# Expert weights of a one-core decoder trunk stored in pairs of blocks and loaded 2 MB at a time

## The chip, the cores and the metric

The kernel runs on one core of one Trainium2 chip. The time is the device time of an execution in microseconds (us): from the first to the last instruction, and the little that lies around that. TensorE (PE in the profile, PEld its weight loads), VectorE (DVE), ScalarE (ACT), GpSimd (POOL) and SyncE (SP) run their own streams of instructions and wait for each other by semaphores. SP issues almost all DMAs, and 16 DMA engines move their data.

## The reference

A decoder trunk of two layers on 256 tokens with a width of 1024, in float32. Layer 0 is latent attention and a dense SwiGLU, layer 1 a diagonal state-space mixer (S5) and a mixture of 8 experts, of which each token takes two:

```python
def moe_swiglu(h, w_router, w_gate, w_up, w_down):
    t = h.reshape(B * S, D)
    logits = (t @ w_router).astype(jnp.float32)
    top_vals, top_idx = lax.top_k(logits, TOP_K)
    gates = jax.nn.softmax(top_vals, axis=-1)
    combine = jnp.sum(jax.nn.one_hot(top_idx, N_EXPERTS) * gates[..., None], axis=1)
    for e in range(N_EXPERTS):
        out = out + combine[:, e:e + 1] * swiglu(t, w_gate[e], w_up[e], w_down[e])
```

Each expert has three matrices of 1024 x 3584, 42 MB in float32 (MB stands for 1,048,576 bytes), and all eight are read: 336 MB.

## The kernel before

**Blocks and places.** `pack` (L1575) stores an expert as 42 blocks of 128 partitions x 2048 values, 1 MB each, in rows of 8 KB. Blocks lie in the order of use: a chunk of 512 hidden columns takes four blocks for gate and up (`up`, L1248) and two for down (`down`, L1339). Expert 0 is split otherwise: its first and last chunks have 256 columns, two blocks up and one down. `seq` (L1431) runs up of a chunk, then down of the chunk before it. `fetch` (L190) loads each block into the next place of a list, `self.rings`, and SP issues that load when the place's last reader is done. In the expert stage the list has 18 places of 1 MB (L1496, L1438): six tiles that the S5 mixer used before (`KEEP`: M0 to M3, E and F), two of pool `ring2`, four of `ring`, the two halves of the router's transposed input (`gh`, `gl`), and the four pairs of split tiles (`whi`, `wlo`, 512 KB each), which take a block as two DMAs with rows of 4 KB (L202; the others are issued at L205). The list is rotated and the last six places join it after `dense` (L1288), the first chunk's up. Before that there are twelve.

**Early loads.** During S5 three blocks are loaded into M0, M1 and M2 as soon as steps S1, S3 and S5 have read these tables (`PF`, L50; `early`, L183, issued at L187). SP's stream there also holds the last weights of S5 (`in_s_glu`, L205) and small copies (`tt<-kk`, L902).

**Token slices.** An expert's tokens, at most 96 or 64 (`CAPS`, L83), stand in slices of 32 (three or two). Every block takes 48 matmul records of 32 x 256 with three slices, 32 with two. The experts come as 96, 64, 96, 96, 64, 96, 96, 64. Between experts stand `scatter` and, for each second one, `gather`.

**Split places.** Up to the first chunk of the experts, weights are split into a rounded part `whi` (ACT, L227) and the rest `wlo` (DVE, L229), and `mm3` (L251) takes three matmuls (L253 to L255). `split` (L216) works two to three parts ahead of the matmuls.

The order of instructions on each engine follows the program, with shifts that the tile framework's scheduler makes.

Of the kernel before, what the change touches and what calls it, by code (L numbers as in the profile page):

```python
# [19 lines left out]
P = 128  # L20
# [28 lines left out]
KEEP = ("M0", "M1", "M2", "M3", "E", "F")  # L49
PF = "S1:M0 S3:M1 S5:M2"  # L50
# [26 lines left out]
RING, RING2, LOOK = 4, 2, 2  # L77
# [25 lines left out]
class Trunk:  # L103
    def __init__(self, ctx, tc, a, out):
# [4 lines left out]
        self.rings = [(pool("ring", bufs=RING), "w")] * RING  # L109
# [55 lines left out]
    def plan_moe(self):  # L165
        a = self.a
        self.expert = {}
        u = 100000 * (1 + len(self.parts))
        ups, downs = [], []
        for e in range(NE):  # L170
            n = 0
            for w in CHUNKS[e]:
                ups.append([(e, n + i) for i in range(w // 128)])
                n += w // 128
                downs.append([(e, n + i) for i in range(w // 256)])
                n += w // 256
        for x, y in zip(ups + [[]], [[]] + downs):
            for e, n in x + y:
                u += 1
                src = a["moe_w"][0, n] if e == 0 else (e, n)  # L180
                self.parts += [(u, src, 0, 1024), (u, src, 1024, 2048)]

    def early(self, tag):  # L183
        u, src, _, _ = self.parts[self.marks["moe"] + 2 * self.nearly]
        self.nearly += 1
        t = self.keep.tile([P, UNIT], F32, tag=tag, name="w")
        self.nc.sync.dma_start(t, src)  # L187
        self.units[u] = t

    def fetch(self):  # L190
        while self.seen < min(self.cap, self.ahead + self.reach):
            u, src, c0, c1 = self.parts[self.seen]
            if u not in self.units:
                k = max(p[3] for p in self.parts[self.seen:self.seen + 8] if p[0] == u)
                if isinstance(src, tuple):
                    src = self.chosen(*src)
                q, tag = self.rings[self.nunit % len(self.rings)]
                self.nunit += 1
                if isinstance(tag, tuple):
                    t = [q.tile([P, UNIT // 2], F32, tag=z, name="w") for z in tag]  # L200
                    for i in range(2):
                        self.nc.sync.dma_start(t[i], src[:, i * UNIT // 2:(i + 1) * UNIT // 2])  # L202
                else:
                    t = q.tile([P, UNIT], F32, tag=tag, name="w")
                    self.nc.sync.dma_start(t[:, :k], src)  # L205
                self.units[u] = t
            self.seen += 1

    def chosen(self, e, n):

        if e not in self.expert:
# [4 lines left out]
    def split(self):  # L216
        nc = self.nc
        while self.ahead < min(len(self.parts), self.stop) and self.ahead <= self.pos + self.look:
# [5 lines left out]
            hi = sp.tile([P, 1024], F32R, tag="whi", name="whi")  # L224
            lo = sp.tile([P, 1024], F32R, tag="wlo", name="wlo")
# [17 lines left out]
    def raw(self):  # L243
# [4 lines left out]
        w = self.units[u]  # L248
        return w[c0 // 1024] if isinstance(w, list) else w[:, c0:c1]
# [491 lines left out]
    def s5_tables(self, m, t):  # L741
# [63 lines left out]
        E = self.keep.tile([P, G, NCK], F32, tag="E", name="E")  # L805
        F = self.keep.tile([P, G, NCK], F32, tag="F", name="F")
# [22 lines left out]
        self.M = [self.keep.tile([P, 16, P], F32, tag=f"M{i}", name=f"M{i}") for i in range(4)]  # L829
# [233 lines left out]
    def route(self, h, m, rest):  # L1063
# [15 lines left out]
        self.gbuf = [m.tile([P, KB, 2, P], F32R, tag=n, name=n) for n in ("gh", "gl")]  # L1079
# [109 lines left out]
    def experts(self, h, m, half):  # L1189
# [204 lines left out]
        def spare(name):  # L1394
            while isinstance(self.rings[self.nunit % len(self.rings)][1], tuple):
                self.nunit += 1
            q, tag = self.rings[self.nunit % len(self.rings)]
            self.nunit += 1
            return q.tile([P, UNIT], F32, tag=tag, name=name)
# [33 lines left out]
        if half == 0:  # L1433
# [4 lines left out]
            self.rings = self.rings[i:] + self.rings[:i] + [(m, "gh"), (m, "gl")] + [(q, ("whi", "wlo")) for q in self.sps]  # L1438
# [30 lines left out]
def trunk_kernel(ctx: ExitStack, tc: tile.TileContext, a, out, stage=9):  # L1469
# [20 lines left out]
    with tc.tile_pool(name="moe", bufs=1, reuse_waits="tile") as m, \  # L1490
# [5 lines left out]
        t.rings = [(t.keep, k) for k in KEEP] + [(r2, "w")] * RING2 + t.rings  # L1496
# [6 lines left out]
        t.moe(h, m, rest)  # L1503


def pack(inputs):
# [68 lines left out]
    o["moe_w"] = w  # L1575
# [18 lines left out]
```

## Time and profile before

| what | value |
|---|---|
| median of 3 runs | 1346.38 us (1344.81 to 1353.78) |
| the profiled execution | 1347.12 us, its span 1345.3 us |
| granted TensorE clock, mean | 0.970 |
| PE busy | 1270.8 us (94%) |
| DVE, ACT, POOL busy | 499.1, 314.6, 48.5 us |
| moved by DMA | 424.26 MB (of 1,000,000 bytes), mean 315 GB/s |
| expert weights | 264 DMAs of 1 MB and 144 of 512 KB |

The expert stage is the stretch from about 450 us to the end. The profile gives, for any stretch, each engine's busy time, the mean busy share of the 16 DMA engines and what they moved (GB/s of 10^9 bytes). The share is a sum of packet times, and neighbours overlap a little, so 1.01 or 1.02 is an engine that never rests. PE's busy time counts modelled ends of pipelined matmuls: a busy PE is not a PE at its peak, and its pace is read from the start times of its records.

### The profile page before, as it was taken

Reading aid. Unit: us, or ns where it says so; the run is one execution under the profiler, and the core shown is the slowest. Engines: PE = TensorE matmul, PEld = TensorE weight load, DVE = VectorE, ACT = ScalarE, POOL = GpSimd, SP = SyncE. Lnnn points to the kernel's source line nnn. Section 1 sums busy time; section 2 is a strip of 40 time slices with the busy share of each in tenths; the row PEclk is TensorE's granted clock in tenths of the full one; section 3 lists DMA queues with packets and bytes.
Section 4 is the critical chain, followed back from the end, with each engine's and each line's share of the span. In section 5 each row is a group of like instructions: output and inputs, shape, how many; then the busy total and the mean of one; then the engine's idle time right before and its main releaser. Section 6 shows DMA issues by size and latency. Waiting matters only on the chain. (4 is left out here: it accounts for less than half of the span.)

```text
span 1345.3 us, 39012 instructions
## 1 busy us (share of the span) xinstructions
PE 1270.8 (94%) x17355; PEld 883.4 (66%) x17355; DVE 499.1 (37%) x1088; ACT 314.6 (23%) x628; POOL 48.5 (4%) x89
## 2 busy tenths in 40 slices
PE   6998999999789899999999999999999999999984
PEld 6777999998677676666555665555655555666542
DVE  5875989987878760102011002002102002000202
ACT  5664544455433450100010000001000001000001
POOL 3000000001033100000000000000000000000000
PEclk9989999999976899999999999999999999999998
DMA  7302455554445779999999999999999999999994
GB/s 277 135 33 105 157 188 189 196 177 169 154 112 151 252 278 407 415 414 415 416 416 416 419 412 403 418 410 399 415 419 408 407 411 407 415 407 418 409 398 169
DMA packets 80448, 424.26 MB, mean 315 GB/s; under 512 B 14608, under 2 KB 18448, under 8 KB 39824
## 3 DMA queue, kind: packets, MB, share of 16 engines
q1 hardware_dynamic: 76016, 418.79, 78.5%
q0 software_dynamic: 1024, 1.31, 0.7%
q8 instruction: 138, 2.26, 0.7%
q10 hardware_dynamic: 3232, 1.58, 0.5%
q14 instruction: 38, 0.31, 0.1%
HBM read 417.19 MB, written 1.05 MB: 311 GB/s over the span
## 5 line engine op out<-in xcount | busy, mean ns | idle before, releaser
L1246 PE MATMUL pg<-w,xg 128*32 128x256 f32 (+1 forms) x7168 | 494.1, 378 | 4.9 <-DMA w<-in_moe_w 4.9
L1246 PEld LDWEIGHTS pg<-w,xg 128*32 128x32 f32 x7168 | 264.4, 110 | 159.2 <-issue 11.8
L1336 PE MATMUL py<-w,th 128*32 128x256 f32 x4704 | 281.4, 379 | 5.9 <-DMA w<-in_moe_w 5.7
L1282 DVE TENSOR_TENSOR sl<-pg,sl 128x256 f32<-128x256 f32 (+1 forms) x56 | 23.7, 423 | 671.9 <-ACT sl L1281 671.9
L1246 PE MATMUL pu<-w,xg 128*32 128x256 f32 (+1 forms) x2240 | 230.1, 376 | 1.6 <-issue 1.6
L1336 PEld LDWEIGHTS py<-w,th 128*32 128x32 f32 x4704 | 160.6, 110 | 106.9 <-DMA w<-in_moe_w 6.7
L1281 ACT ACTIVATE sl<-pg 128x256 f32<-128x256 f32 (+1 forms) x56 | 21.4, 383 | 651.9 <-PE pg L1246 651.9
L229 DVE TENSOR_TENSOR wlo<-w,whi 128x1024 fp32r<-128x1024 f32 (+1 forms) x120 | 141.3, 1181 | 45.4 <-ACT whi L227 45.0
L227 ACT CAST whi<-w 128x1024 fp32r<-128x1024 f32 (+1 forms) x120 | 121.6, 1019 | 126.2 <-PE pg L254 52.1
L1246 PEld LDWEIGHTS pu<-w,xg 128*32 128x32 f32 x2240 | 102.1, 110 | 48.8 <-issue 3.0
L254 PE MATMUL pg<-n1l,whi 128*128 128x256 f32 x352 | 101.6, 289 | 0.0
L255 PE MATMUL pg<-n1h,wlo 128*128 128x256 f32 x352 | 101.4, 288 | 0.0
L253 PE MATMUL pg<-n1h,whi 128*128 128x256 f32 x352 | 101.3, 288 | 0.1
L253 PEld LDWEIGHTS pg<-n1h,whi 128*128 128x128 f32 x352 | 67.4, 192 | 1.2 <-ACT whi L227 0.3
L254 PEld LDWEIGHTS pg<-n1l,whi 128*128 128x128 f32 x352 | 67.5, 192 | 0.7
L255 PEld LDWEIGHTS pg<-n1h,wlo 128*128 128x128 f32 x352 | 67.4, 192 | 0.0
L253 PE MATMUL fo<-whi,th 128*128 128x512 f32 x88 | 34.6, 393 | 0.3 <-ACT th L700 0.3
L254 PE MATMUL fo<-wlo,th 128*128 128x512 f32 x88 | 34.5, 392 | 0.0
L255 PE MATMUL fo<-whi,tl 128*128 128x512 f32 x88 | 34.3, 389 | 0.0
L1423 POOL TENSOR_TENSOR fx<-h,gF 128x512 f32<-128x512 f32 x1 | 1.3, 1266 | 881.1 <-DVE h L1421 881.1
L1284 DVE STREAM_TRANSPOSE th<-sl 128x384 f32<-128x384 f32 (+2 forms) x56 | 29.4, 525 | 2.0
L1223 ACT ACTIVATE xg<-pgt,prm 128x192 f32<-128x192 f32 x32 | 11.7, 418 | 62.6 <-PE pgt L1218 62.6
(478 smaller groups left out, 1396.1 us busy)
## 6 DMA issues: line engine op xcount, KB each, us to landing
w<-in_moe_w SPq DMA_DIRECT2D x264, 1024.0 KB, 17.1
w<-in_moe_w SPq DMA_DIRECT2D x144, 512.0 KB, 13.6
w<-in_ffn_gu SPq DMA_DIRECT2D x22, 1024.0 KB, 4.8
w<-in_ffn_dn SPq DMA_DIRECT2D x11, 1024.0 KB, 4.8
w<-in_s_glu SPq DMA_DIRECT2D x8, 1024.0 KB, 5.8
w<-in_mla_o SPq DMA_DIRECT2D x4, 1024.0 KB, 4.8
w<-in_s_in SPq DMA_DIRECT2D x4, 1024.0 KB, 4.7
w<-in_mla_in SPq DMA_DIRECT2D x4, 672.0 KB, 8.9
```

The source lines that it names most:

```text
L227: nc.scalar.copy(hi[:, :k], w[:, c0:c1])
L229: self.lo_dve = nc.vector.tensor_sub(lo[:, :k], w[:, c0:c1], hi[:, :k].bitcast(F32))
L253: mm(out, lhsT=lh, rhs=rh, start=first, stop=False)
L254: mm(out, lhsT=lh, rhs=rl, start=False, stop=False)
L255: mm(out, lhsT=ll, rhs=rh, start=False, stop=last)
L1223: self.g_act = nc.scalar.activation(x[:, q + i], src, AF.Copy, scale=gc)
L1246: mm(ps[t // 2][32 * q:32 * q + 32, t % 2, 0:w], lhsT=lhsT, rhs=rhs[:, q], start=first and t % 2 == 0, stop=last and (t % 2 == 1 or t == n ...
L1281: self.silu = nc.scalar.activation(sl[:, ts], src[:, :, 0:k], AF.Silu)
L1282: v.tensor_tensor(sl[:, ts], src[:, :, k:2 * k], sl[:, ts], op=ALU.mult)
L1284: v.transpose(th.rearrange("p t b x -> p (t b x)"), sl.rearrange("p t k -> p (t k)"))
L1336: mm(y[e][b][32 * q:32 * q + 32, i, :], lhsT=th[:, t, fb], rhs=w[:, c * 256:(c + 1) * 256], start=first and i == 0, stop=last and (nt == 2 ...
L1423: (nc.gpsimd, v)[n if XM else 1].tensor_mul(x[:, 1, s], h[:, 1, s], gF[:, s])
```

## The change

- `pack` stores two consecutive blocks side by side, in rows of 16 KB. In expert 0 the two single down blocks are moved behind the others, so that the rest pairs up (`stored`).
- The places become five double ones of 2 MB (M0 with M1: `MA`; M2 with M3: `MB`; E with F: `EF`; one of `ring2`; `gh` with `gl`: `gg`) and eight single ones: four of `ring`, and the four split places, in each of which `whi` and `wlo` are now the halves of one tile `ws`.
- A double place takes a pair in one DMA. A single place, or a double one that meets the second block of a pair or a block of no pair, takes half a pair: rows of 8 KB out of 16.
- Two pairs are loaded early, after S3 and S7, in place of three blocks after S1, S3 and S5.

```diff
-KEEP = ("M0", "M1", "M2", "M3", "E", "F")
-PF = "S1:M0 S3:M1 S5:M2"
+KEEP = ("MA", "MB", "EF")
+PF = "S3:MA S7:MB"
-RING, RING2, LOOK = 4, 2, 2
+RING, RING2, LOOK = 4, 1, 2
...
+    def place(self, name="w"):
+        q, tag, n = self.rings[self.nunit % len(self.rings)]
+        self.nunit += 1
+        return q.tile([P, n * UNIT], F32, tag=tag, name=name), n
...
     def early(self, tag):
-        t = self.keep.tile([P, UNIT], F32, tag=tag, name="w")
-        self.nc.sync.dma_start(t, src)
-        self.units[u] = t
+        t = self.keep.tile([P, 2 * UNIT], F32, tag=tag, name="w")
+        self.nc.sync.dma_start(t, self.chosen(e, k))
+        self.units[u], self.units[u + 1] = t[:, 0:UNIT], t[:, UNIT:2 * UNIT]
...
+                    e, p, i, pair = src
+                    src = self.chosen(e, p)
+                    if pair and n == 2:
+                        self.nc.sync.dma_start(t, src)
+                        self.units[u], self.units[u + 1] = t[:, 0:UNIT], t[:, UNIT:2 * UNIT]
+                    else:
+                        self.units[u] = t[:, 0:UNIT]
+                        self.nc.sync.dma_start(t[:, 0:UNIT], src[:, i * UNIT:(i + 1) * UNIT])
...
-            hi = sp.tile([P, 1024], F32R, tag="whi", name="whi")
-            lo = sp.tile([P, 1024], F32R, tag="wlo", name="wlo")
+            ws = sp.tile([P, UNIT], F32R, tag="ws", name="ws")
+            hi, lo = ws[:, 0:1024], ws[:, 1024:UNIT]
...
-            self.rings = self.rings[i:] + self.rings[:i] + [(m, "gh"), (m, "gl")] + [(q, ("whi", "wlo")) for q in self.sps]
+            self.rings = self.rings[i:] + self.rings[:i] + [(m, "gg", 2)] + [(q, "ws", 1) for q in self.sps]
...
-        t.rings = [(t.keep, k) for k in KEEP] + [(r2, "w")] * RING2 + t.rings
+        t.rings = [(t.keep, k, 2) for k in KEEP] + [(r2, "w", 2)] * RING2 + t.rings
...
+def stored(e):
+
+    return [n for n in range(NUNIT) if e or n not in (2, NUNIT - 1)] + ([] if e else [2, NUNIT - 1])
...
-    o["moe_w"] = w
+    o["moe_w"] = c(np.stack([w[e][stored(e)].reshape(NUNIT // 2, 2, P, UNIT).transpose(0, 2, 1, 3).reshape(NUNIT // 2, P, 2 * UNIT) for e in range(NE)]))
```

## Rows read from the trace of the kernel before

**Rows 1.** Busy time by stretch: the expert stage
```profile
core 0: us, PE busy (x) PEld busy (x) DVE busy (x) ACT busy (x) POOL busy (x), PEclk, DMA share, GB/s
505.00:1320.00 815.00, 801.76 (x14114) 476.94 (x14106) 97.46 (x216) 58.56 (x153) 0.00 (x0) 1.00 1.01 411
```
**Rows 2.** Matmuls of the last blocks, in order of time
```profile
start us, us, engine line op out<-in xcount [idle before <-releaser]
...
1323.02 1.93 PE L1336 MATMUL py<-w,th 128*32 128x256 f32 x32 [0.59 <-DMA w<-in_moe_w]
1325.39 1.93 PE L1336 MATMUL py<-w,th 128*32 128x256 f32 x32 [0.43 <-DMA w<-in_moe_w]
```
**Rows 3.** Busy time of L1246 (PE, PEld) by expert: 1, 2, 4 and 7
```profile
608.00:689.70 81.70, 54.76 (x915) 31.59 (x910) 1.00 1.01 417
689.90:802.70 112.80, 79.41 (x1379) 45.85 (x1374) 1.00 1.02 415
...
923.30:1002.60 79.30, 51.69 (x870) 29.63 (x864) 1.00 1.01 412
...
1238.10:1326.90 88.80, 48.57 (x806) 26.31 (x798) 1.00 0.96 386
```
**Rows 4.** Matmuls of expert 1 (two slices): two downs, one chunk apart
```profile
625.78 3.61 PE L1336 MATMUL py<-w,th 128*32 128x256 f32 x60
...
636.14 3.61 PE L1336 MATMUL py<-w,th 128*32 128x256 f32 x60
```
**Rows 5.** SP's waits, 510 to 600 us
```profile
engine line waited for: us in total, times, longest us
SPq L205 <- PE pu L1246: 43.1, 20, 2.9
SPq L205 <- PE py L1336: 14.0, 7, 2.2
```
**Rows 6.** DMA issues (KB each, median us to landing); a DMA queue (packets, MB, share)
```profile
w<-in_moe_w SPq DMA_DIRECT2D x264, 1024.0 KB, 17.1
w<-in_moe_w SPq DMA_DIRECT2D x144, 512.0 KB, 13.6
...
q8 instruction: 138, 2.26, 0.7%
```
**Rows 7.** Busy time by stretch: rows of 8 KB, then of 4 KB
```profile
516.00:548.00 32.00, 32.00 (x600) 19.30 (x596) 3.44 (x13) 4.09 (x7) 0.00 (x0) 1.00 1.01 421
549.00:561.00 12.00, 12.00 (x228) 7.27 (x224) 1.20 (x3) 0.66 (x2) 0.00 (x0) 1.00 1.02 407
```
**Rows 8.** Busy time by stretch: a slow piece of the stream
```profile
828.00:836.00 8.00, 8.00 (x156) 4.82 (x152) 0.95 (x3) 0.05 (x1) 0.00 (x0) 1.00 0.96 355
```
**Rows 9.** Busy time by stretch: before the first expert chunk
```profile
480.00:504.00 24.00, 23.51 (x179) 17.17 (x182) 15.21 (x61) 13.91 (x32) 0.00 (x0) 1.00 0.64 221
```
**Rows 10.** SP's issues around the end of S5, in order of time
```profile
398.53 0.33 SPq L187 DMA_DIRECT2D w<-in_moe_w  x1
...
438.83 10.84 SPq L902 DMA_DIRECT2D tt<-kk  x8
449.72 2.54 SPq L205 DMA_DIRECT2D w<-in_s_glu  x2
...
453.26 31.87 SPq L205 DMA_DIRECT2D w<-in_moe_w  x10
489.85 3.81 SPq L202 DMA_DIRECT2D w<-in_moe_w  x4
```
**Rows 11.** The weight split: groups of the page (busy, mean ns, idle before)
```profile
L227 ACT CAST whi<-w 128x1024 fp32r<-128x1024 f32 (+1 forms) x120 | 121.6, 1019 | 126.2 <-PE pg L254 52.1
...
L255 PE MATMUL pg<-n1h,wlo 128*128 128x256 f32 x352 | 101.4, 288 | 0.0
...
L253 PEld LDWEIGHTS pg<-n1h,whi 128*128 128x128 f32 x352 | 67.4, 192 | 1.2 <-ACT whi L227 0.3
```

More of the change, by code (lines that the diff above doesn't have):

```diff
@@ L108, in __init__ @@
         self.small = pool("small", bufs=2)
-        self.rings = [(pool("ring", bufs=RING), "w")] * RING
+        self.rings = [(pool("ring", bufs=RING), "w", 1)] * RING
         self.nunit, self.lo_gate = 0, None
@@ L165, in plan_moe @@
     def plan_moe(self):
-        a = self.a
         self.expert = {}
@@ L194, in fetch @@
                 k = max(p[3] for p in self.parts[self.seen:self.seen + 8] if p[0] == u)
[L195 to L202, printed above, removed]
-                else:
-                    t = q.tile([P, UNIT], F32, tag=tag, name="w")
-                    self.nc.sync.dma_start(t[:, :k], src)
-                self.units[u] = t
+                t, n = self.place()
+                if not isinstance(src, tuple):
+                    self.units[u] = t
+                    self.nc.sync.dma_start(t[:, :k], src)
+                else:
+                    e, p, i, pair = src
[6 more added lines that the diff above has]
+                        self.nc.sync.dma_start(t[:, 0:UNIT], src[:, i * UNIT:(i + 1) * UNIT])
             self.seen += 1
     def chosen(self, e, n):
+        if e == 0:
+            return self.a["moe_w"][0, n]
         if e not in self.expert:
@@ L247, in raw @@
         self.pos += 1
-        w = self.units[u]
-        return w[c0 // 1024] if isinstance(w, list) else w[:, c0:c1]
+        return self.units[u][:, c0:c1]
     def mm3(self, out, lh, ll, rh, rl, first, last):
@@ L804, in s5_tables @@
         yield
-        E = self.keep.tile([P, G, NCK], F32, tag="E", name="E")
-        F = self.keep.tile([P, G, NCK], F32, tag="F", name="F")
+        EF = self.keep.tile([P, 2, G, NCK], F32, tag=KEEP[2], name="EF")
+        E, F = EF[:, 0], EF[:, 1]
         self.E, self.F = E, F
@@ L828, in s5_tables @@
                             yield
-        self.M = [self.keep.tile([P, 16, P], F32, tag=f"M{i}", name=f"M{i}") for i in range(4)]
+        M = [self.keep.tile([P, 2, 16, P], F32, tag=z, name=z) for z in KEEP[0:2]]
+        self.M = [M[i // 2][:, i % 2] for i in range(4)]
         for b in range(8):
@@ L1078, in route @@
         nc.gpsimd.tensor_copy(tri, self.cst[:, C_TRI:C_TRI + P])
-        self.gbuf = [m.tile([P, KB, 2, P], F32R, tag=n, name=n) for n in ("gh", "gl")]
+        gg = m.tile([P, 2, KB, 2, P], F32R, tag="gg", name="gg")
+        self.gbuf = [gg[:, 0], gg[:, 1]]
         xh, xl = self.x3 = [z.rearrange("p k a t -> p k (a t)") for z in self.gbuf]
@@ L1394, in spare @@
         def spare(name):
[L1395 to L1399, printed above, removed]
+            return self.place(name)[0][:, 0:UNIT]
         def final_start():
```

13 lines of the change are left out of this document (6 added, 7 removed).

## The prediction, made before the change was run

> **What bounds the kernel now.** I read the strip of 40 slices first: from about 500 us on the DMA row stands at 9 to the last slice. So the busy time by stretch comes next: from 505 to 1320 us the DMA engines' share is 1.01, at 411 GB/s, and the clock is 1.00 [rows 1]. 411 GB/s are 2.551 us per MB, and the stream never rests. PE is busy all the time as well, so the third view has to be its pace. Per expert [rows 3], one of three slices takes 112.8 us (expert 2), 2.69 us per MB, slower than the stream. One of two slices can go faster: from one down to the next, which is one chunk or 6 MB, expert 1 takes 636.14 - 625.78 = 10.36 us, 1.73 us per MB [rows 4]. So the blocks in SBUF pile up in three-slice experts and are eaten in two-slice ones. Where the pile is gone PE goes at the stream's pace: each group of matmuls for the last blocks has 0.4 to 0.6 us of idle before it, released by a weight DMA [rows 2]. Expert 7 takes 88.8 us, where 42 MB at 1.73 us and some 3.5 us for the scatter (an estimate: what expert 2's 112.8 us leave over 42 MB at 1.5 x 1.73, three slices for two) make 76. Expert 4 takes 79.3. PE thus waits for data some 13 + 3 = 16 us, and the execution ends when the stream does. That is the limit for any gain from the stream: 1347.1 - 16 = 1331 us.
>
> SP's waits show the other end of the pile: in expert 0 SP waits 57 of 90 us for PE to give places back [rows 5], while the stream, with its issued loads, still runs.
>
> **The loads themselves.** In a stretch that moves rows of 8 KB alone the stream makes 421 GB/s, in one of 4 KB rows (the split places) 407 [rows 7]. Per row on one of 16 engines that is 8192 x 16 / 421 = 311.3 ns and 4096 x 16 / 407 = 161.0 ns: 150.3 ns for 4 KB more, and 10.7 ns for each row whatever its size. A row of 16 KB on the same line is 611.9 ns, so 2 MB (eight rows per engine) take 4.895 us, 2.448 us per MB; 1 MB in 8 KB rows takes 2.491, in 4 KB rows 2.576.
>
> Before: 264 x 2.491 + 72 x 2.576 = 843.1 us [rows 6]. After: a lap of 13 places holds 18 blocks, five pairs and eight single; 336 blocks are 18.7 laps, so 93 pairs and 150 single: 93 x 4.895 + 150 x 2.491 = 828.9 us. The difference is 14.2 us. 16 of the 336 MB lie before 505 us, where the stream is not the limit, which leaves 13.5. 72 x 0.085 = 6.1 us of the 14.2 come from the 4 KB rows that go, 186 x 0.043 = 8.0 from the 16 KB rows.
>
> No row shows a weight load of 16 KB rows, so its price has two ends. Below: no cost per row, 601 ns, 8 us more gained. Above: the only queue with packets of that size, the instruction queue (2.26 MB in 138), has 0.007 x 16 x 1345 / 138 = 1.09 us per packet [rows 6], which would add 93 x 3.8 = 355 us. Its packets share the engines with weight packets, which would be in their time too; I take the line through the two sizes of the same queue. Between the ends stands a row cut into two packets of 8 KB, 2.491 us per MB.
>
> The stream's slow pieces stay as they are: 355 GB/s over 8 us [rows 8], and the 13 us between 815 us and the 802 that 320 MB would take at the rates of [rows 7]. Nothing in the change touches them.
>
> What the Trainium skill says of a load's fixed cost ("DMA: Bandwidth & Descriptors", the anatomy of one DMA on the SWDGE path) is about 2.0 us for each, whatever its size. The change issues 165 DMAs less, so by that sentence alone it would save up to 330 us. The trace disagrees for this queue: loads take 13.6 and 17.1 us to land while the share stays at 1.01 [rows 1, 6], so what is fixed lies under other loads. If the 0.085 us per MB between the two rates of [rows 7] belonged to the additional DMA and not to the shorter rows, 165 fewer would save 14.0 us, the same sum.
>
> **The start.** From 480 to 504 us the share is 0.64 [rows 9]: 8.6 us of rest, because places are full. The change takes one place from this stretch: block 6, expert 0's single down, sits alone in the double `ring2` place, so 11 blocks fit where 12 did. And `MA` comes free only when both its blocks are split, which is when the last of the ten issues of [rows 10] went out (453.26 + 31.87 = 485.1), and not one block earlier as M0 did. Against it stands one more MB loaded early. About 4.5 us more rest, 2.5 less to load: 2 us lost. Bounds: 2.5 gained (the places give the same rest as now) to 5 lost (`MB`, which needs two blocks of the first chunk consumed, holds SP's queue up).
>
> **The end.** The last two blocks are one pair now. After its landing 64 records remain where 32 do now: 1.9 us [rows 2] minus the wait saved, 1.7 us lost. Below zero it cannot go; the bound above is one load, 2.5.
>
> **Early loads in S5.** Two loads of 4.9 us at S3 and S7 replace three of 2.5 at S1, S3 and S5. The one at S7 lands on SP's queue beside the last copies (438.83 to 449.67) and before two S5 weights at 449.72 [rows 10], which wait behind it for up to 4.9 us. Their split begins later than that, and PE works on earlier parts meanwhile. I take 0; bounds 2.5 gained (a load less beside the small copies) and 4.9 lost if that cover is gone.
>
> **Joined split places.** ACT waits for the place 52.1 us in all, released by L254, the last reader of `whi` [rows 11]. With one tile it is released by L255, at most 288 ns later, in 44 parts of the dense layer: 12.7 us if nothing covered it. PE's weight load of `whi` shows 1.2 us of idle in all 352, so two parts in advance cover it: 0. Fewer issues on SP: 0, it waits anyway.
>
> **Sum.** -13.5 + 2 + 1.7 = -9.8 us on the profiled execution's 1347.1: 1337.3. That execution is 0.7 us above the median, so I say 1337. PE has 16 us to give, and 9.8 are taken: the end stays with the stream.
>
> **Rivals.**
> A, the forecast, 1337 (its own range 1331 to 1343): chance 0.52.
> B, 16 KB rows move as two packets: 336 x 2.491 = 837.0, 5.8 us saved after 505 us, less 3.7 lost: 1345. For it: no 16 KB row of this queue is seen. Against: the instruction queue has packets of that size. 0.13.
> C, the long rows cost nothing per row, or the start loses nothing: the stream runs away and PE's own pace ends it, 1331. Against: [rows 7] show a cost per row. 0.13.
> D, slower: depth. A double place comes back only when both blocks are used, and a pair can be used only when 2 MB have landed. That is about 0.5 MB held, 1 MB later, 1 MB in the half-empty place: 2.5 to 3 MB less of a pile of 18, 7.5 us at 2.5 us per MB in each of the two eating stages (experts 4 and 7), 15 us: 1337 + 15 = 1352. For it: SP waits for places in expert 0 already [rows 5]. Against: the stream's share stays at 1.0 there. It decides once the pile at the start of expert 4 is under some 12 MB. 0.15.
> E, slower: longer rows meet in memory. Neighbouring partitions lie 16 KB apart, so the engines' streams are 64 KB apart where they were 32. If pairs went at the 355 GB/s of [rows 8], each would take 5.91 us in place of 4.90: 93 x 1.01 = 94 us, 1431; it costs more than it gives from 5.05 us a pair on. Against: half blocks of 4 KB at a pitch of 8 KB go at 407, on the line. 0.07.
> The skill's same page, under latency and other measured facts, has such a loss for row pitches from 512 KiB up (207 GB/s there, 103 at 4 MiB), far above 16 KB; no run here shows it.
>
> **Chances and range.** A measurement tells about 1% from no change here: 1333 and 1360 are the marks. Faster by more: C mostly (0.10) and A's lower end (0.08), 0.18. Slower by more: E and a bad D, 0.09. Within: 0.73. The range 1329 to 1353 holds A, B, C and most of D.
>
> **What would show it.** Right: DMA share 1.0 from 505 us on; 428 GB/s where pairs alone move and 421 in single places, none at 407; 93 issues of 2 MB and 150 of 1 MB; expert 4 at 76 to 77 us, expert 7 near 80; PE's waits for weights halved. Rest in 480 to 504 of about 13 us. Wrong: a rate of 421 throughout with twice the packets (B); shares under 0.95 in expert 0 or more than 16 us of PE waits (D); under 415 GB/s in stretches of pairs (E); first expert matmul later than 501 us (the S5 loads).

## The result, and the profile after

The changed kernel takes 1357.49 us (median of 15 runs, 1353.05 to 1360.94), the kernel before 1348.36 us beside it (15 runs, 1344.81 to 1354.08). The ratio is 1.0065, with a 95% interval of 1.0052 to 1.0079: slower by some 9 us, where 10 us less was forecast. The profiled execution after takes 1353.05 us, the lowest of its 15, with a span of 1351.3 us; the span before is 1345.3, so the two profiles differ by 6.0 us where the medians differ by 9.1.

The stream of weights did nearly what the change wanted. Busy time by stretch, for the stretches of [rows 9], [rows 1] and [rows 7], and the first 80 us after these:

```profile
480.00:504.00 24.00, 24.00 (x127) 17.69 (x126) 17.89 (x63) 11.61 (x24) 0.00 (x0) 1.00 0.57 201
505.00:1320.00 815.00, 808.49 (x14188) 485.23 (x14191) 100.86 (x222) 65.44 (x168) 0.00 (x0) 1.00 1.00 416
516.00:548.00 32.00, 32.00 (x580) 19.24 (x571) 3.03 (x8) 2.29 (x7) 0.00 (x0) 1.00 1.00 411
...
520.00:600.00 80.00, 80.00 (x1481) 48.00 (x1473) 8.49 (x27) 7.33 (x16) 0.00 (x0) 1.00 0.99 404
```

The whole stage goes from 411 to 416 GB/s, though its beginning is slower (404 GB/s from 520 to 600 us; this is the line before):

```profile
520.00:600.00 80.00, 78.38 (x1547) 49.03 (x1539) 7.04 (x22) 6.08 (x13) 0.00 (x0) 1.00 1.01 417
```

The DMA issues of the page, to be held against [rows 6], and the packets between 505 and 1320 us (56011 before):

```profile
w<-in_moe_w SPq DMA_DIRECT2D x93, 2048.0 KB, 23.0
w<-in_moe_w SPq DMA_DIRECT2D x150, 1024.0 KB, 22.8
```

```profile
DMA packets 33672, 338.70 MB, mean 416 GB/s; under 512 B 3735, under 2 KB 3735, under 8 KB 3799
```

93 pairs and 150 single blocks, as counted. In this stretch 89 pairs and 142 singles are issued, at 128 rows each 29568 packets; with the 3.8 thousand small ones that makes 33.4 of the view's 33.7 thousand. A row of 16 KB is one packet. The experts, busy time of L1253 by stretch, for experts 1, 2, 4 and 7 as in [rows 3]:

```profile
618.70:700.70 82.00, 54.15 (x915) 31.74 (x911) 1.00 1.00 421
700.90:813.70 112.80, 79.41 (x1380) 45.86 (x1374) 1.00 1.01 422
933.50:1014.30 80.80, 53.10 (x868) 30.27 (x864) 0.98 1.01 421
1248.40:1332.30 83.90, 48.34 (x806) 25.48 (x798) 0.96 0.89 370
```

The stream makes 421 to 422 GB/s where it made 412 to 417. Expert 7 falls from 88.8 to 83.9 us, expert 4 does not fall (79.3 to 80.8). PE's waits for weights, 4.9 + 5.7 us on the page before, are halved, as the page's groups show (after the bar busy time, mean ns, idle before):

```profile
L1253 PE MATMUL pg<-w,xg 128*32 128x256 f32 (+1 forms) x7168 | 494.3, 379 | 2.5 <-DMA w<-in_moe_w 2.5
...
L1343 PE MATMUL py<-w,th 128*32 128x256 f32 x4704 | 280.6, 381 | 2.7 <-DMA w<-in_moe_w 2.7
...
L233 ACT CAST ws<-w 128x1024 fp32r<-128x1024 f32 (+1 forms) x120 | 121.5, 1019 | 123.6 <-PE pg L260 31.2
...
L258 PEld LDWEIGHTS pg<-n1h,ws 128*128 128x128 f32 x352 | 67.3, 191 | 1.4 <-ACT ws L233 0.5
```

The last two lines answer to [rows 11]: the joined split tile is released by L260, the last reader of `lo`, and nothing waits noticeably longer for it.

So the loss lies ahead of the stage. The first expert matmul starts at 500.4 us before and at 511.5 after; the last ends at 1327.3 and 1332.6. The stage is thus 5.8 us shorter (826.9 to 821.1), and all else is lost earlier. In S5, counted from block 0's output (its first `py<-tt` matmul, 377.4 and 374.4 us; other profiled executions here have it between 374 and 380) to the first expert matmul, 123.0 us became 137.1. SP's issues in that stretch, to be held against [rows 10]:

```profile
start us, us, engine line op out<-in xcount [idle before <-releaser]
394.55 0.33 SPq L190 DMA_DIRECT2D w<-in_moe_w  x1
404.06 4.91 SPq L908 DMA_DIRECT2D tt<-kk  x4
413.44 0.33 SPq L874 DMA_DIRECT2D bc<-in_s5bc  x1
416.48 0.33 SPq L876 DMA_DIRECT2D dd<-in_s_dd  x1
416.86 0.67 SPq L874 DMA_DIRECT2D bc<-in_s5bc  x1
...
431.81 2.52 SPq L908 DMA_DIRECT2D tt<-kk  x4
...
445.84 0.33 SPq L190 DMA_DIRECT2D w<-in_moe_w  x1
446.41 10.34 SPq L908 DMA_DIRECT2D tt<-kk  x8
457.21 0.34 SPq L201 DMA_DIRECT2D w<-in_s_glu  x1
```

Two things are to be seen. Each early load of 2 MB stands directly ahead of small copies (`tt<-kk`, the local operators of the S5 blocks). And the loads of table rows (`bc`, L874), one of which SP issued at 402.26 us before, ahead of block 3's copies, now stand behind them at 413.44 us. SP's issues before, behind the early load of 398.53 us [rows 10]:

```profile
402.26 0.33 SPq L868 DMA_DIRECT2D bc<-in_s5bc  x1
402.64 0.42 SPq L205 DMA_DIRECT2D w<-in_s_glu  x1
405.90 4.94 SPq L902 DMA_DIRECT2D tt<-kk  x4
```

Two of SP's longest waits in the changed kernel, from 374 to 470 us:

```profile
engine line waited for: us in total, times, longest us
...
SPq L908 <- DMA X<-ut: 12.2, 4, 9.0
...
SPq L190 <- PE pS L937: 9.6, 1, 9.6
```

The early load at S7 is at the head of SP's queue for 9.6 us until PE has read `MB`, with the last eight copies behind it. And the copies of block 3 wait 9.0 us at the head for small copies of ScalarE's queue (`X<-ut`), which were issued beside the first load. How long DMAs took from issue to landing, 394 to 404 us in the changed kernel:

```profile
w<-in_moe_w SPq DMA_DIRECT2D x1, 2048.0 KB, 8.3
X<-ut ACTq DMA_DIRECT2D x8, 16.0 KB, 6.8
tt<-kk POOLq DMA_DIRECT2D x1, 64.0 KB, 4.2
```

PE stands still for them, in order of time:

```profile
402.08 1.06 PE L928 MATMUL pU<-cst,X 32*128 32x32 f32 x8 [5.66 <-DMA w<-in_moe_w]
```

The matmul belongs to block 4 and reads `X`. The last of the eight copies that fill this `X` was issued at 394.62 us, 0.07 us behind the load, and took 7.1 us, to 401.7. (The profile names the load as what ended the wait, but that landed only at 402.9.) Before, the same matmul waited for the same copy for 1.04 us:

```profile
399.24 1.04 PE L922 MATMUL pU<-cst,X 32*128 32x32 f32 x8 [1.04 <-DMA X<-ut]
```

### The profile page after: what moved, and what is told of

Its sections match the earlier page's. It is cut to its first block, busy times and chain, and to the rows that moved or that the text cites. A ratio compares the mean times of both kernels' runs of the same rounds, so it can differ in the third digit from the quotient of the medians.

```text
span 1351.3 us, 38357 instructions
## 1 busy us (share of the span) xinstructions
PE 1270.0 (94%) x17355; PEld 885.0 (65%) x17355; DVE 499.9 (37%) x1088; ACT 314.1 (23%) x628; POOL 47.9 (4%) x89
## 3 DMA queue, kind: packets, MB, share of 16 engines
q0 software_dynamic: 1024, 1.31, 0.6%
## 5 line engine op out<-in xcount | busy, mean ns | idle before, releaser
L1253 PE MATMUL pg<-w,xg 128*32 128x256 f32 (+1 forms) x7168 | 494.3, 379 | 2.5 <-DMA w<-in_moe_w 2.5
L1253 PEld LDWEIGHTS pg<-w,xg 128*32 128x32 f32 x7168 | 264.9, 110 | 157.6 <-issue 12.5
L1253 PE MATMUL pu<-w,xg 128*32 128x256 f32 (+1 forms) x2240 | 230.9, 377 | 1.4 <-issue 1.4
L1343 PEld LDWEIGHTS py<-w,th 128*32 128x32 f32 x4704 | 163.5, 110 | 100.9 <-issue 4.4
L235 DVE TENSOR_TENSOR ws<-w,ws 128x1024 fp32r<-128x1024 f32 (+1 forms) x120 | 141.4, 1184 | 42.4 <-ACT ws L233 41.7
L233 ACT CAST ws<-w 128x1024 fp32r<-128x1024 f32 (+1 forms) x120 | 121.5, 1019 | 123.6 <-PE pg L260 31.2
L1253 PEld LDWEIGHTS pu<-w,xg 128*32 128x32 f32 x2240 | 102.4, 110 | 49.1 <-issue 3.4
L259 PE MATMUL pg<-n1l,ws 128*128 128x256 f32 x352 | 101.5, 288 | 0.0
L260 PE MATMUL pg<-n1h,ws 128*128 128x256 f32 x352 | 101.4, 288 | 0.0
L258 PE MATMUL pg<-n1h,ws 128*128 128x256 f32 x352 | 101.1, 287 | 0.3 <-ACT ws L233 0.3
L258 PEld LDWEIGHTS pg<-n1h,ws 128*128 128x128 f32 x352 | 67.3, 191 | 1.4 <-ACT ws L233 0.5
L259 PEld LDWEIGHTS pg<-n1l,ws 128*128 128x128 f32 x352 | 67.3, 191 | 0.7
L260 PEld LDWEIGHTS pg<-n1h,ws 128*128 128x128 f32 x352 | 67.3, 191 | 0.0
L258 PE MATMUL fo<-ws,th 128*128 128x512 f32 x88 | 34.5, 392 | 0.0
L259 PE MATMUL fo<-ws,th 128*128 128x512 f32 x88 | 34.5, 392 | 0.0
L260 PE MATMUL fo<-ws,tl 128*128 128x512 f32 x88 | 34.3, 390 | 0.0
```

The source lines that it names most:

```text
L233: nc.scalar.copy(hi[:, :k], w[:, c0:c1])
L235: self.lo_dve = nc.vector.tensor_sub(lo[:, :k], w[:, c0:c1], hi[:, :k].bitcast(F32))
L258: mm(out, lhsT=lh, rhs=rh, start=first, stop=False)
L259: mm(out, lhsT=lh, rhs=rl, start=False, stop=False)
L260: mm(out, lhsT=ll, rhs=rh, start=False, stop=last)
L1253: mm(ps[t // 2][32 * q:32 * q + 32, t % 2, 0:w], lhsT=lhsT, rhs=rhs[:, q], start=first and t % 2 == 0, stop=last and (t % 2 == 1 or t == n ...
```

## The experiments

Theory T1: the two early loads lengthen S5. Rival T2: the joined tiles and the order of instructions that came with them do, whatever is loaded. T3: S5 aside, the half-empty and late places at the start of the stage eat the gain. T4 and T5 came when T1 had to be split: by order (table loads behind copies) or by bytes (small copies landing behind 2 MB). All lengths below are from the profiled execution of each kernel, read from its timeline in the same way; times are medians, ratios are against the kernel before run beside it.

| kernel | time, us | ratio, 95% interval | S5, us | stage, us |
|---|---|---|---|---|
| before | 1348.4 | 1 | 123.0 | 826.9 |
| changed | 1357.5 | 1.0065 (1.0052 to 1.0079) | 137.1 | 821.1 |
| changed, no early loads | 1339.4 | 0.9938 (0.9914 to 0.9962) | 120.0 | 822.6 |
| before, four early loads of 1 MB | 1356.3 | 1.0072 (1.0047 to 1.0096) | 130.5 | 825.7 |
| changed, first four places single | 1346.0 | 0.9985 (0.9970 to 1.0000) | 124.2 | 822.0 |
| before, no early loads | 1352.9 | 1.0033 (1.0016 to 1.0051) | 124.0 | 830.1 |
| changed, S3 load only | 1355.7 | 1.0048 (1.0028 to 1.0068) | 137.4 | 820.9 |
| changed, early loads in halves | 1355.5 | 1.0041 (1.0015 to 1.0067) | 142.3 | 818.7 |
| no early loads, pairs in halves | 1345.1 | 0.9984 (0.9968 to 1.0001) | 124.2 | 825.1 |
| before, split places joined | 1341.9 | 0.9951 (0.9932 to 0.9971) | 125.2 | 819.7 |
| changed, a quarter of each early load | 1344.8 | 0.9975 (0.9952 to 0.9997) | 126.8 | 821.7 |
| changed, table loads by GpSimd | 1346.8 | 0.9977 (0.9964 to 0.9991) | 128.8 | 822.5 |
| no early loads, ring2 one step later | 1346.5 | 0.9976 (0.9963 to 0.9989) | 122.7 | 826.4 |
| changed, 1 MB at S3 | 1353.0 | 1.0036 (1.0018 to 1.0053) | 136.5 | 821.0 |
| changed, S3 load, the others held back | 1350.2 | 1.0007 (0.9995 to 1.0020) | 131.6 | 821.0 |
| changed, all held back | 1339.9 | 0.9935 (0.9919 to 0.9952) | 120.6 | 822.0 |
| no early loads, last pair in halves | 1337.5 | 0.9920 (0.9897 to 0.9943) | 121.4 | 817.6 |
| before, joined, no early loads | 1344.9 | 0.9975 (0.9956 to 0.9993) | 126.1 | 821.3 |

The S5 and stage columns come from one execution each. Four kernels have no early load and the same order of SP's issues in S5 (the changed kernel without early loads, and the same with pairs in halves, with `ring2` one step later, with the last pair in halves): their S5 takes 120.0, 124.2, 122.7 and 121.4 us. Differences of up to some 4 us in these columns are not resolved.

### Is it the early loads?

**The changed kernel without early loads.**

```diff
-PF = "S3:MA S7:MB"
+PF = ""
```

> The changed kernel without its two early loads of 2 MB (all expert blocks are loaded from the end of S5 on). T1 (the two loads cost some 15 us of S5, by the lanes and the place in SP's order): the first expert matmul comes back from 511.5 to about 497-501 us; 4 MB less are loaded by then, at most 9.8 us at 2.45 us per MB, part of it in rest, so the total is 1344 to 1353. T2 (the rearranged tiles and order of S5 cost it, whatever is loaded early): first expert matmul at 508 us or later, total 1357 to 1367.

1339.4 us, S5 120.0 us, first expert matmul at 498.0 us. T2 falls, and the time is below that of both kernels. The total lies even under T1's range: 18 us for two loads. One thing differs from the text above: the first pair did not wait for the end of S5. The scheduler let SP issue it at 418.89 us, between the copies of blocks 4 and 5, and there it did no harm.

**The kernel before without its three.**

```diff
-PF = "S1:M0 S3:M1 S5:M2"
+PF = ""
```

> The kernel before without its three early loads. It is the measure for what early loads are worth in S5 and after it. If early loads cost S5 nothing (what the prediction took): first expert matmul at 500 us or later, and up to 3 x 2.5 = 7.5 us more at the end, 1349 to 1355. If the three loads of 1 MB cost S5 too: first expert matmul 3 to 8 us earlier, total 1344 to 1349.

1352.9 us, the first of the two cases: early loads of 1 MB at S1, S3 and S5 cost S5 nothing (123.0 us with, 124.0 without) and are worth 4.7 us. (Here too one block went out within S5, at 420.93 us.)

**The kernel before with four early loads of 1 MB, named at S3 and S7.**

```diff
-PF = "S1:M0 S3:M1 S5:M2"
+PF = "S3:M0 S3:M1 S7:M2 S7:M3"
```

> The kernel before, with four early loads of 1 MB, two each at S3 and S7, where the changed kernel loads its pairs. T1, if amount and place count and not the 16 KB rows: first expert matmul 505 to 512 us (500.4 before), total 1349 to 1359. T1, if it takes one DMA of 2 MB to hold a lane and the engines: 500 to 503 us and a total of 1345 to 1349. T2: unchanged, 500 us, total 1346 to 1348, since the tiles and their order are those of before.

1356.3 us, first matmul at 506.6 us: a total as slow as the changed kernel's, with rows of 8 KB and single places, and in the range of the first case. But the loads did not go out in twos: SP issued them at 380.67, 395.52, 420.31 and 445.85 us. So 1 MB, and not 2, stood at the place of each early pair, ahead of block 3's copies (both table loads behind these, at 408.64 and 410.08 us) and ahead of the last eight. S5 lost 7.5 us of the 14.1 that it lost in the changed kernel; the stage, with the split places of before, gained only 1.2 of its 5.8 us. The run shows that early loads at these places cost S5 time without pairs, long rows or joined tiles; it does not show that 2 MB do.

**The changed kernel with its early loads issued as halves.**

```diff
-        self.nc.sync.dma_start(t, self.chosen(e, k))
+        for i in range(2):
+            self.nc.sync.dma_start(t[:, i * UNIT:(i + 1) * UNIT], self.chosen(e, k)[:, i * UNIT:(i + 1) * UNIT])
```

> The changed kernel with each of the two early loads issued as two DMAs of 1 MB in rows of 8 KB, at the same two points. If the size of one DMA counts (a lane held for 2 MB, packets of 16 KB in front of small copies): first expert matmul at 505 to 508 us, as in the kernel before with four early loads at these points (506.6), total 1350 to 1354. If only the amount and the point in S5 count: 510 to 513 us, 1356 to 1360.

1355.5 us, S5 142.3 us (first matmul 519.2, later than either case). The loss is there without a DMA of 2 MB and without rows of 16 KB, so it needs neither. The points are not quite the same: the scheduler put block 3's copies between the halves of the first pair (396.13 and 409.83 us), and both table loads behind the second half (415.98 and 419.23 us).

### What each load costs

**The load at S3 alone, first attempt.** `PF = "S3:MA"`.

> The changed kernel with the early load of 2 MB at S3 alone; the one at S7 goes, and its two blocks are loaded with the others after S5. Without either the first expert matmul stands at 498.0 us (total 1339.4), with both at 511.5 (1357.5). If each of the two costs its share (the small copies behind it, then SP's queue): 503 to 507 us and 1344 to 1350. If the one at S7 costs nearly all, by SP's 9.7 us wait with the last copies behind it: 498 to 501 us, 1337 to 1341. If the one at S3 costs nearly all, through the order of everything behind it: 508 us or later, 1351 to 1358.

1355.7 us and 514.5 us, which reads as if S3 cost all. It does not follow: SP issued the second pair at 448.82 us, again directly ahead of the last eight copies, the same place as at S7. The run separated nothing.

**The S3 load, with the others held back**, and **all held back**: no other expert load is issued before the last small copy of block 7.

```diff
+                if b == 7 and AQ[jj] not in "pa":
+                    self.gate = z
...
-                        self.nc.sync.dma_start(t, src)
+                        with self.behind(self.gate if e == 0 and p < 2 else None):
+                            self.nc.sync.dma_start(t, src)
```

> The changed kernel with the early load of 2 MB at S3, and every other expert load held back on SP until block 7's last small copy is issued, so that no load stands in front of the copies of blocks 6 and 7 (in the run with the S3 load alone SP issued the second pair at 448.8 us, ahead of those eight copies, just as at S7). Blocks in the traces so far put some 9.5 of the 14 us that S5 lost at the S3 load (by block 5) and 4.5 at the second one (blocks 6 and 7). If so: S5's length from block 0's output to the first expert matmul 131 to 134 us (123.0 before, 137.1 changed), first matmul at 507 to 511 us, total 1348 to 1353. If the S3 load costs it all: 136 us or more, total 1354 to 1358. If the second load costs it all: 122 to 126 us, total 1339 to 1345.

> The changed kernel with no expert load before block 7's last small copy (the kernel without early loads still issued its first pair at 418.9 us, between the copies of blocks 4 and 5). If that 2 MB load at 418.9 us cost S5 nothing: S5's length 119 to 121 us as there (120.0), and 2 MB less loaded, so the total is 1339 to 1344. If it cost something too: S5 2 to 5 us shorter, total 1336 to 1340.

S5 is 131.6 us with the S3 load and 120.6 with none, both as their first cases have it. The S3 load costs 11.0 us of S5, the second one 137.1 - 131.6 = 5.5, each known to some 4 us; in the medians 10.3 and 7.3. The 2 MB at 418.89 us cost nothing (120.0 against 120.6), and bring nothing either (1339.4 us in all against 1339.9). SP's issues with all held back, the same stretch of the program as above:

```profile
397.71 2.69 SPq L875 DMA_DIRECT2D bc<-in_s5bc  x2
402.04 2.89 SPq L909 DMA_DIRECT2D tt<-kk  x4
...
412.67 0.33 SPq L875 DMA_DIRECT2D bc<-in_s5bc  x1
415.48 3.92 SPq L909 DMA_DIRECT2D tt<-kk  x4
...
437.23 10.12 SPq L909 DMA_DIRECT2D tt<-kk  x8
```

Both table loads go out ahead of block 3's copies. And the small copies there, 397 to 404 us, land in 2 us where they took 4 to 7:

```profile
bc<-in_s5bc SPq DMA_DIRECT2D x2, 256.0 KB, 2.6
X<-ut ACTq DMA_DIRECT2D x10, 16.0 KB, 2.1
tt<-kk POOLq DMA_DIRECT2D x1, 64.0 KB, 2.4
```

For the second load, the last copies (issue to landing) with it ahead of them, 445 to 457 us of the changed kernel, and then with the loads held back, 450 to 460 us of the run with the S3 load alone:

```profile
w<-in_moe_w SPq DMA_DIRECT2D x1, 2048.0 KB, 10.3
tt<-kk POOLq DMA_DIRECT2D x2, 64.0 KB, 7.9
...
tt<-kk SPq DMA_DIRECT2D x2, 8.0 KB, 9.3
```

```profile
tt<-kk POOLq DMA_DIRECT2D x2, 64.0 KB, 2.9
...
tt<-kk SPq DMA_DIRECT2D x2, 8.0 KB, 2.4
```

An 8 KB copy takes 9.3 us behind the load and 2.4 without it. It is this landing that costs, and not the 9.6 us that the load waits at the head of SP's queue: the last eight copies start 72.0 us after block 0's output in the changed kernel (446.41 us) and 72.9 us after it with the load held back (451.72 us).

### Order or bytes

**A quarter of the bytes, the same order.** 512 KB at S3 and S7; `fetch` loads the other 1.5 MB of each pair when it comes to it.

```diff
-        self.nc.sync.dma_start(t, self.chosen(e, k))
-        self.units[u], self.units[u + 1] = t[:, 0:UNIT], t[:, UNIT:2 * UNIT]
+        self.nc.sync.dma_start(t[:, 0:1024], self.chosen(e, k)[:, 0:1024])
+        self.begun[u] = t
```

> The changed kernel with a quarter of each early load at its old point: 512 KB at S3 and S7 (4 KB of each 16 KB row); the other 1.5 MB of each pair goes out with the blocks that follow. SP's order through S5 stays that of the changed kernel, with the load of block 5's table rows behind the copies of block 3. T4 (order: what S5 lost, it lost because the table loads of blocks 5 and 6 stand behind small copies that wait): first expert matmul at 507 to 512 us, total 1353 to 1358. T5 (bytes: the 2 MB in front of the small copies held them and the queue's semaphores): 498 to 503 us and 1340 to 1346. Both in part: between.

1344.8 us, S5 126.8: T5's range. With SP's order unchanged, 12.7 of the 17.6 us between 1357.5 and 1339.9 are back. The table loads stand behind the copies as before, but go out at 404.25 and 408.02 us in place of 413.44 and 416.86, and the `X` copies land in 2.7 us (median of 11) and not in 6.8. (The rest of the first pair went out at 431.44 us, behind the copies of block 5.)

**The table loads on GpSimd's queue, all bytes as in the changed kernel.**

```diff
-            nc.sync.dma_start(bc, a["s5bc"][b])
+            nc.gpsimd.dma_start(bc, a["s5bc"][b])
```

> The changed kernel with its early loads of 2 MB at S3 and S7 as they are, and the S5 table loads (eight of 256 KB) issued by GpSimd in place of SP, so that they don't stand in SP's order. T4 (order): S5 gets back nearly all, first expert matmul at 498 to 503 us, total 1339 to 1346. T5 (bytes): the small copies still land behind 2 MB, first matmul at 507 to 512 us, 1353 to 1358. If GpSimd's queue is itself late for the tables, S5 is longer than both.

1346.8 us, S5 128.8: a little above T4's range. It can't be read as order alone, since SP also issued the second pair only at 450.35 us here, behind the last copies; it is to be compared with the S3 load by itself. There block 5's output starts 69.6 us after block 0's (58.7 with all held back, 59.7 to 62.5 in the four kernels without early loads named above); with the tables freed, 62.0. By block 7 only 2.6 of these 7.6 us are left (84.7 against 87.3; 76.3 with all held back). Why the rest went again, the run doesn't tell.

**Half of the S3 load's bytes, the same order.** As the quarter, with `UNIT` for 1024 and S3 alone.

> As the kernel with the early load at S3 alone (1355.7 us, first expert matmul 514.5), with half of its bytes at that point: 1 MB, 8 KB of each 16 KB row, the amount that the kernel before loads there; the other half goes out with the blocks that follow, 35 us later. SP's order stays that of the changed kernel. If the loss follows the bytes in front of the small copies (13 us between 512 KB and 2 MB): about a third of it, first matmul at 503 to 508 us, total 1344 to 1350. If it is a step (the copies slip past a point, and the tables behind them with it), 1 MB costs nearly all or nearly nothing: 509 us or later and 1352 to 1358, or 498 to 502 us and 1339 to 1344.

1353.0 us, first matmul 510.9: 1 MB at S3 costs nearly as much as 2 MB, the step of the second case. Block 5 starts 67.4 us after block 0 (67.9 changed; 61.6 with 512 KB, which is no more than some kernels without early loads have). But a whole pair was issued at 445.69 us ahead of the last copies again, so some 5 us of the loss are the second load's; the figure at block 5 lies ahead of it. The kernel before loads the same 1 MB at S3 for nothing, with a table load right behind it at 402.26 us, ahead of block 3's copies. So bytes do not do it alone. The reading that fits is that bytes and order act together: bytes make the small copies land late, and what stands behind these on SP is late by that. It is argued and not isolated, because a second order differs too. Before, the load at S3 goes out 2.2 us after block 4's last `X` copy (396.34 us, landed in 2.5 us); in the changed kernel 0.07 us ahead of it, and that copy takes 4.2, 5.6 and 7.1 us behind 512 KB, 1 MB and 2 MB. No run moves the load by that alone.

### The stream

**The split places joined, alone, in the kernel before.**

```diff
-            hi = sp.tile([P, 1024], F32R, tag="whi", name="whi")
-            lo = sp.tile([P, 1024], F32R, tag="wlo", name="wlo")
+            ws = sp.tile([P, UNIT], F32R, tag="ws", name="ws")
+            hi, lo = ws[:, 0:1024], ws[:, 1024:UNIT]
...
-... [(q, ("whi", "wlo")) for q in self.sps]
+... [(q, "ws") for q in self.sps]
```

(The lines left out make the two DMAs of such a place one.)

> The kernel before with its split places joined, and nothing else: one tile of 1 MB for both halves, so an expert block there is one DMA in 8 KB rows in place of two in 4 KB rows; early loads, places and storage as before. The line of the prediction: 72 blocks by 0.085 us = 6.1 us less, 1341 to 1343. If the joined tile's later release costs ACT (44 parts by up to 0.29 us in the dense layer) or the stream is not the bound: 1346 to 1350.

1341.9 us, 6.5 less; the line said 6.1.

**No early loads, each pair as two DMAs of 8 KB rows into its double place.**

> The changed kernel without early loads (1339.4 us), and each pair loaded as two DMAs of 1 MB in rows of 8 KB into the same double place. It measures the term of the long rows by itself. The line of the prediction (10.7 ns for each row): 186 blocks by 0.043 us = 8.0 us more, some 7 to 9, 1346 to 1349. If long rows give nothing and the whole gain lies in the joined split places: 1338 to 1341. If the pairs' late return of places costs as much as the rows give, blocks that come one by one would give some of it back: 1341 to 1345.

1345.1 us, 5.7 more than 1339.4: between the second and first case, against 8.0 by the line. From 505 to 1300 us the stream makes 415 GB/s here, 419 in the kernels with whole pairs and no early loads, and 416 and 417 in the two with joined tiles and no pairs (the next run, and the one above): 2 to 4 GB/s, or 4 to 8 us in 795. The long rows raise the rate, by the line's 8 us at most.

**Joined, without early loads and without pairs** (the kernel with joined split places alone, with `PF = ""`).

> The kernel before with its split places joined and no early loads: all places single, all rows 8 KB. Against the changed kernel without early loads (1339.4 and 1339.9 us) it has no pairs, no double places and no 16 KB rows. If the long rows give the 8.0 us of the prediction, or the 5.7 that halves in the double places showed: 1345 to 1348. If the double places take back what the long rows give (start, late return, last pair): 1338 to 1342. Below 1338 the double places would cost more than the rows give.

1344.9 us, 5.4 more than the changed kernel without early loads, on the edge of the first case. So pairs and double places are worth 5 to 6 us net, from two sides. (Its profiled execution, the longest of six, has 126.1 us of S5 and a stage of 821.3, no longer than the 822.6 and 822.0 with pairs, and so puts the difference into S5; the lengths of single executions don't settle where it lies.)

**The first four places single.** `M0` to `M3` are single tiles and places, loaded early as before, each block half a pair.

```diff
-KEEP = ("MA", "MB", "EF")
-PF = "S3:MA S7:MB"
+KEEP = ("M0", "M1", "M2", "M3", "EF")
+PF = "S1:M0 S3:M1 S5:M2"
```

> The changed kernel with the first four places single again and the early loads as before: three halves of a pair, 1 MB each in 8 KB rows, at S1, S3 and S5; EF, ring2 and gg stay double, so three pairs in a lap of 18 blocks instead of five. T1: first expert matmul 499 to 502 us; the stream keeps 14.2 us less two fifths of the 8.0 us of the long rows, some 11 us, so the total is 1338 to 1343, faster than before. T2: first expert matmul 508 us or later, total 1353 to 1360. T3 (the start is dry for the half-empty double place and the late return of places, not for S5): first matmul at 500, but total still 1346 or more.

1346.0 us, T3's edge by its number. S5 is back (124.2 us), as T1 says; the stream did not gain, because only 22 pairs were issued as pairs: in this list most double places meet the second block of a pair. A slip of the experiment, and no evidence for T3.

**No early loads, `ring2` behind the first single place.**

```diff
-        t.rings = [(t.keep, k, 2) for k in KEEP] + [(r2, "w", 2)] * RING2 + t.rings
+        t.rings = [(t.keep, k, 2) for k in KEEP] + t.rings[:1] + [(r2, "w", 2)] * RING2 + t.rings[1:]
```

> The changed kernel without early loads (1339.4 us), and the double place of ring2 one step later in the list, behind the first single place. Expert 0's single down takes that single place, so no double place of the first lap before dense is half empty (12 blocks fit by then in place of 11), and the last two blocks of the stream come one by one. If the start and the end are what is left of the loss (2.5 and 1.7 us at most): 1335 to 1338. If neither is on the path any more, or another place is half empty later: 1339 to 1342.

1346.5 us, worse than both cases, for the same reason: 65 pairs were issued where 93 were. The half-empty place of the first lap is part of what keeps the later pairs in step.

**No early loads, the last pair of the stream as two DMAs.**

> The changed kernel without early loads (1339.4 us), and the last pair of the stream as two DMAs of 1 MB. The term of the end: from the last weight packet to the last expert matmul 1.2 us before, 3.0 changed, 4.7 in the kernel without early loads. If the late landing of the last 2 MB costs it: 1.2 us again there, and 1 to 3.5 us less in all, 1336 to 1338.5. If the stream's own end comes later by as much, no change: 1339 to 1341.

1337.5 us, ratio 0.9920: the fastest kernel of the study, some 11 us under the one before and 20 under the changed one. Against 1339.4 it is 1.9 us, and the two intervals overlap. The last matmuls of the stream, in the kernel without early loads and with the last pair halved, show the mechanism ([rows 2] has them before). Behind each stands the busy time by stretch around them, whose last numbers are the granted clock, the DMA share and GB/s:

```profile
1315.19 5.35 PE L1343 MATMUL py<-w,th 128*32 128x256 f32 x64 [2.50 <-DMA w<-in_moe_w]
```

```profile
1315.00:1321.00 6.00, 5.81 (x69) 3.73 (x70) 0.41 (x1) 0.37 (x1) 0.00 (x0) 0.72 0.01 3
```

```profile
1310.94 1.93 PE L1344 MATMUL py<-w,th 128*32 128x256 f32 x32 [0.62 <-DMA w<-in_moe_w]
1313.32 1.93 PE L1344 MATMUL py<-w,th 128*32 128x256 f32 x32 [0.44 <-DMA w<-in_moe_w]
```

```profile
1308.00:1316.00 8.00, 6.55 (x104) 3.76 (x106) 0.42 (x1) 0.37 (x1) 0.00 (x0) 1.00 0.34 140
```

64 records wait 2.50 us for all of 2 MB; with halves the first 32 run while the second half is under way. And the 64 are slower, 84 ns each against 60: after the longer wait the granted clock of the stretch is 0.72, so part of it ran at the lower of the two levels (1.2 GHz); with halves it is 1.00.

## Why the prediction was wrong

**Early loads in S5: the step that failed.** It took 0 us, with bounds of 2.5 gained and 4.9 lost. Measured: 10.3 us for the one at S3 and 7.3 for the one at S7 in the medians (S5 by 11.0 and 5.5), 17.6 together. Three slips are in it. It weighed each load by what waits for the load's own bandwidth, 4.9 us, and only against the two S5 weights behind the second. It put the S7 load beside the last copies [rows 10], while in the changed kernel's order it stands ahead of all eight, which then land in 5.9 to 9.3 us and not in 2.0 to 3.1. And it gave the S3 load no row at all, though [rows 10] had the one of 1 MB before at 398.53 us; what stood behind it (a table load, block 3's copies) was in the same view, between the lines that [rows 10] shows. S5 is a chain of blocks handed through small copies, tables and PE; a copy that lands 5 us later is not hidden by other blocks for long. The sign "first expert matmul later than 501 us" was named and came true, at 511.5 us. That the two loads cost these microseconds is shown by holding them back; how the cost of the one at S3 divides between its bytes and the two orders (table loads, block 4's last `X` copy) stays open. No rival had this step: D, the slower one, put its 15 us into the stage, and it is luck that its 1352 lies nearer to 1357.5 than the forecast.

**The stream, 13.5 us.** Right in size. Joined places: 6.1 forecast, 6.5 measured (8.0 without early loads, 1352.9 - 1344.9). Long rows: 8.0 forecast; the times show 5.4 and 5.7, the rates 4 to 8. Rival B (two packets a row) falls by the packet count, rival E (meeting in memory) by 421 to 422 GB/s where the mix of a lap, (10 x 2.448 + 8 x 2.491) / 18 = 2.467 us per MB, makes 425. Without early loads, the change as a whole is worth 1352.9 - 1339.9 = 13.0 us. That is net of the start and the end: by the prediction's own terms it would be 13.5 - 4.5 - 1.7 = 7.3, so the start cost less than its term, or the stream gave more.

**The start, 2 us lost, and rival D.** Not separated from the rest. The rest from 480 to 504 us is 10.3 us (share 0.57), where some 13 were forecast and 8.6 stood before. The changed kernel runs at 404 GB/s from 520 to 600 us, where 417 were made before; at 425 it would have moved the same in 80 x 404 / 425 = 76 us, 4 us less. It is not the places alone: the kernel with all loads held back has the same ones and makes 421 in that stretch, two others without early loads (none early, last pair in halves) 412 and 411. These places are in the fastest kernel too, so T3 does not explain the loss. D's price of 15 us in the stage is not there: the stage became shorter by 5.8 us. That depth costs something elsewhere wasn't tried.

**The end, 1.7 us.** The mechanism is right, the size by the trace too small: it counted 32 records more, 1.9 us, while the last 64 take 5.35 us where the last 32 took 1.93, 3.4 us more, in the changed kernel as in the one without early loads. The clock that falls in the longer wait (0.72 above) was in no term. The 1.9 us that came back in the medians when the last pair was split can't tell 1.7 from 3.4.

**The early loads' worth.** The prediction counted one MB more loaded early as 2.5 us won. The three before are worth 4.7 us; the two pairs bring no visible gain in the stage (821.1 us with both, 821.0 with one, 822.0 with none), where the DMA engines rest for want of places in each of these kernels (share 0.57 with both and 0.56 with none from 480 to 504 us).

**Split tiles and SP's issues at 0.** Right by the groups above and by the run with joined places alone.

The sum without the failed step, -9.8 us, stands beside what the kernel gives with the loads held back: 1339.9 against 1348.3 beside it, -8.4. That they are so close is in part luck: the sum counts on early loads, one MB more than before, and the kernel with the loads held back has none, while the one before has three that are worth 4.7 us.

## What to carry to other kernels

Before a transfer is moved or enlarged, list every DMA that any queue issues in the length of its landing, and ask for each who waits for it: a copy of 8 KB can wait for 2 MB of somebody else's data. A prefetch is to be priced by what it stands in front of, in the issue order that the changed program will have and not in the old one; holding all prefetches back until the last small copy was out won 17.6 us against the changed kernel. It is the place that counts and not the prefetch as such: three loads of 1 MB at other points were worth 4.7 us to the kernel before. And an experiment that drops an early load has to be read for where the scheduler puts that load instead.

## What was not expected of the hardware

Small copies on one engine's queue land late behind a large load on another's. `X<-ut` copies of 16 KB, issued by ScalarE, take 2.1 us with no load beside them, 2.7 us beside 512 KB, 3.5 beside 1 MB (3.7 in the kernel before, beside two loads of 1 MB), and 6.8 beside 2 MB on SP's queue, which itself takes 8.3 (medians); `tt<-kk` copies of GpSimd's queue go from 2.9 to 7.9 us beside the second load. A separate queue did not protect them here. The copies' packets themselves waited, as the queues show (packets, MB, share of the engines), first from 395.5 to 401 us of the changed kernel, then from 401 to 404; q1 is SP's, here with the load in rows of 16 KB, q10 ScalarE's with the `X` copies in rows of 512 bytes:

```profile
q1 hardware_dynamic: 120, 1.97, 101.2%
q10 hardware_dynamic: 40, 0.02, 1.1%
```

```profile
q10 hardware_dynamic: 296, 0.10, 13.7%
q1 hardware_dynamic: 24, 0.13, 10.6%
```

While the load moves, q10 gets 40 packets through, and 296 in the 3 us in which it ends. The Trainium skill, "DMA: Bandwidth & Descriptors", section on queues, rings and completion order, has two rules that bear on it: a DMA engine changes between queues only at packet boundaries, and the write that raises a DMA's semaphore lands only after every earlier write of that engine, from whichever queue. The second can't be all of it, since the data moved late and not only its signal; and the first `X` copy behind the load landed at 401.7 us, ahead of the load at 402.9, so a copy need not wait for the whole of a load that was issued before it. Whether the first rule makes these counts, no run here shows.

The line through two row sizes gave the sign and nearly the size for a third: 407 and 421 GB/s at 4 and 8 KB [rows 7], 425 by the line for a lap's mix with 16 KB rows, and 421 to 422 measured in experts 1, 2 and 4, without a penalty for pitch or packet. From 505 to 1300 us, slow pieces included, it is 419 with pairs against 415 to 417 without.
